# Hybrid decoder layer on one core: input-projection pairs placed ahead of the last three whole gates, PSUM pools closed one stage later, one more group of MLP operands made during the output projection

## The chip, the core and the metric

The kernel runs on one core of a Trainium2 chip. The core's engines work from queues of their own, each in order: TensorE (PE, matmuls; PEld is its weight load), VectorE (DVE), ScalarE (ACT), GpSimd (POOL) and SyncE (SP), which here issues every DMA. The metric is the device time of one execution in microseconds (us). Times inside an execution come from a profile of one execution, counted from its first instruction.

## The reference

One decoder layer over 1024 tokens, model width 1024, float32 in and out:

```python
h = h + hybrid_mixer(rms_norm(h, norm1_g), w_in, conv_w, conv_norm_g, ret_norm_g, w_out)
h = h + sq_relu_mlp(rms_norm(h, norm2_g), w_up, w_down)
return rms_norm(h, final_norm_g)
```

`hybrid_mixer` multiplies by `w_in` (1024 x 3584) and cuts the result into three convolution groups of 512 columns (b, c, h) and four retention groups of 512 (q, k, v, gate). The first give `b * causal_dwconv3(c * h)` and a group norm over 64 channels; the second a chunkwise retention in 4 heads of 128 with rotary q and k, a norm per head, and a product with `silu(gate)`. The 1024 columns that come out are multiplied by `w_out`. The MLP is `relu(u @ w_up)^2 @ w_down` with an inner width of 4096.

## The kernel before

Everything is kept transposed: 128 channels on the partitions, tokens along the row. Most tiles are 128 x 1024 float32 and come from one pool of 40 buffers ("units", `unit()`). A product in float32 precision is made of three products of rounded halves: an operand is split into a high half (ACT casts it) and a low half (DVE or POOL subtracts), and PE forms high x high, high x low and low x high. A piece of weights, 512 rows x 128 columns, is loaded by SP into a raw tile `r` (`Stream.fetch`, 4 buffers in the mixer), cast by ACT into `wh` and subtracted into `wl` (`split_piece`). `prepare()` does this for the next piece; it is called once per product or every other quarter of a whole tile, and pieces run four ahead of PE. `wh` and `wl` have 4 buffers each, so a cast can wait for PE to be done with an older piece. 12 matmuls of 128 x 512 make one product or one step.

The stages, with their places in the profiled execution: value projection and norm of the input (to 54 us); q and k tiles, then the first whole tiles, with the retention running beside them (to about 235 us); the pairs of input tiles (to 327 us); the last two gates, `IN_END` (to 350 us); the output projection (359 to 448 us); the first MLP products, `early` (448 to 496 us); six cycles of up and down products (to about 1031 us); the last down products and the final norm (to 1087 us).

Input tiles: numbers 0 to 11 are the convolution's (group i has 3i, 3i+1, 3i+2), 12 to 19 q and k, 20 to 23 the gates of heads 0 to 3. `whole(f)` makes one tile in 48 matmuls into two banks. `pair_in((f, g))` makes two tiles by seven block products instead of eight (a Strassen-like scheme, in the order `UP_ORDER`), 84 matmuls; it needs sums of weight blocks (`Left.split`, POOL) and sums of input blocks ("t1" to "t4", in `U`), and DVE adds each product from its bank into the outputs, seven additions in all. `use` then starts the rest for each half row: `conv_h`, `conv_b` with its norm (`norm`, two small matmuls with `blkr`), or `gate` (z * R, SiLU on ACT, product with the head's output).

The order of the background work is a planner's at build time: `now` counts PE's time in slots of 2.72 us, `clock` holds each engine's modelled end, and `background` emits a waiting task's next step once an engine would start it within `LOOK` = 3.2 us. PE's own order and `prepare` are fixed by the loops.

Because units are short, the outputs of heads 2 and 3 and the first two convolution outputs are written to DRAM (`put_by`, pool `spill`) and read back (`get_back`, tiles `back`) when the pairs are done. A task `split_y` waits for `y[idx]` (for idx 0 and 1 also for the key `("back", idx)`) and splits one half row into `y_h`, `y_l`. In `IN_END` the gates 22 and 23 are made first for half 0 and then for half 1, so that half 0 of all y can be split while half 1 is still on PE.

[...] The mixer has two pools of four, `pm` and `pr`; they belong to the `mixer` stack and are closed with it ahead of the output projection, where the pools `pu` (2), `pd` (4) and `pn` (2) are opened. `group(j)` makes output tiles j and 4 + j in eight steps: first half row 0 (both tiles, `w_out` rows 0 to 511, then 512 to 1023), then half row 1. `out_evac` adds the bank to the residual `x2`, squares it for the norm, and scales it into `un`. `todo` holds, by step number 8j + s, what is made for the MLP beside it: the seven operands "11", "21", "t1", "t3", "t2", "22", "t4" of each j (high half by ACT, low half by DVE), sums (`sum1` to `sum4`, DVE), `put_aside` (an `x2` tile to DRAM). For j = 0 and 1 all seven are made in the projection; for j = 2 and 3 the last four are made in `rest`, beside the 14 early products, which run in the order 11, 21, t2, t1, 22, t3, t4, each for two blocks. `fetch_back` reads tiles put aside, and `new_basis(i)` (POOL) subtracts part of `x2[i]` from `x2[i-1]` and `x2[i]`.

Nearly every DVE, ACT and POOL instruction is recorded under line 73, the call inside the planner's `Engine`; the profile tells them apart by their tiles.

Of the kernel before, what the change touches and what calls it, by code (L numbers as in the profile page):

```python
# [14 lines left out]
PSUM = bass.MemoryType.PSUM  # L15
# [21 lines left out]


IN_QK = [12, 13, 16, 17, 14, 15, 18, 19]
IN_TURNS = [0, 1, 2, 3, 20, (4, 5), (6, 7), 21, (8, 9), (10, 11)]  # L40
IN_END = [22, 23]
SLOT, LOOK, PE_MARGIN, LATE = 2.72, 3.2, 1.2, 0.0
NORM_MARGIN, STEP_MARGIN = 4.0, 0.3
# [35 lines left out]
def hybrid_layer(  # L79
# [16 lines left out]
    now, clock, procs, got = [0.0], {}, [], {}  # L96
    act = Engine(nc.scalar, 0.13, 0.95, now, clock)
    pool = Engine(nc.gpsimd, 0.2, 2.5, now, clock)
    dve = Engine(nc.vector, 0.13, 1.04, now, clock, pool)
# [4 lines left out]
    rw = ctx.enter_context(tc.tile_pool(name="rw", bufs=4))  # L104
    wp = ctx.enter_context(tc.tile_pool(name="wp", bufs=4))
    mixer = ctx.enter_context(ExitStack())
    pm = mixer.enter_context(tc.tile_pool(name="pm", bufs=4, space=PSUM))
    pr = mixer.enter_context(tc.tile_pool(name="pr", bufs=4, space=PSUM))
    tp = mixer.enter_context(tc.tile_pool(name="tp", bufs=6))
    xp = mixer.enter_context(tc.tile_pool(name="xp", bufs=1))  # L110

# [8 lines left out]
    def unit(dt=F32, s="u"):  # L120
        return big.tile([P, T], dt, tag="u", name=nm(s))
# [63 lines left out]
    IN_ORDER = list(IN_QK)  # L185
    for turn in IN_TURNS + IN_END:
        IN_ORDER += turn if isinstance(turn, tuple) else [turn]
# [37 lines left out]
    ahead = 3  # L225
    for turn in IN_TURNS + IN_END:
        if isinstance(turn, tuple):
            o = Left(mix, 1)
# [183 lines left out]
    def spawn(gen, ready=None, late=0.0):  # L412
        Task(gen, now[0] if ready is None else ready, late).go()
# [39 lines left out]
    def force(key):  # L453
        while key not in got:
            background(1e9)
            assert key in got, key

    y, y_h, y_l = [None] * KT, [None] * KT, [None] * KT
# [106 lines left out]
    o_n, retention_task = {}, [None, None]  # L565
# [165 lines left out]
    def whole(f):  # L731
        def evac(z):
            if f < 20 and f % 3 == 0:
                out = a_of[f // 3] = unit(s="a")
                for half, sl in enumerate(hs):
                    act.copy(out[:, sl], z[half])
                return
            out = None if f < 20 and f % 3 == 1 else unit(s="z")
            for half in range(2):
                spawn(use(f, half, out, z[half], True), clock[dve])  # L740

        tile_in(evac)
# [14 lines left out]
    def put_hi(name, j, src):  # L757
        u = unit(F32R, "U")
        act.copy(u[:, :H], src)
        U.setdefault(name, [None] * 4)[j] = (u[:, :H], u[:, H:])  # L760
# [93 lines left out]
    def put_by(key, of, *ready):  # L854
        for r in ready:
            yield r
        yield (dve,)
        t = of()
        spilt[key] = spill.tile([P, T], F32, tag="sp", name=nm("sp"))
        nc.sync.dma_start(spilt[key], t)  # L860
        mark(("by", key), dve)

    def get_back(key):
        t = unit(s="back")
        nc.sync.dma_start(t, spilt.pop(key))
        return t
# [12 lines left out]
        spawn(put_by(("o", h), lambda h=h: o_n[h, 0], ("o", h, 1)))  # L879
    for i in range(2):  # L880
        spawn(put_by(("y", i), lambda i=i: y[i], ("y", i, 0), ("y", i, 1)))
    for turn in IN_TURNS:
        if isinstance(turn, tuple):
            pair_in(turn)
        else:
            whole(turn)
    for h in (2, 3):
        force(("by", ("o", h)))
        o_n[h, 0] = o_n[h, 1] = get_back(("o", h))
    for i in range(2):  # L890
        force(("by", ("y", i)))
        y[i] = get_back(("y", i))
        got["back", i] = now[0] + 5.0
    for idx in range(KT):
        spawn(split_y(idx, 0))
    ends = {f: (unit(s="z"), [bank() for _ in hs], []) for f in IN_END}
# [32 lines left out]
        nc.sync.dma_start(x2[i], xT[i * P : (i + 1) * P, :])  # L929
    un = [None] * 4  # L930
    mixer.close()
    pm = ctx.enter_context(tc.tile_pool(name="pu", bufs=2, space=PSUM))
    pr = ctx.enter_context(tc.tile_pool(name="pd", bufs=4, space=PSUM))
    pn = ctx.enter_context(tc.tile_pool(name="pn", bufs=2, space=PSUM))
    ct = ctx.enter_context(tc.tile_pool(name="ct", bufs=11))
    kept = ctx.enter_context(tc.tile_pool(name="kept", bufs=5, space=bass.MemoryType.DRAM))
    rv = ctx.enter_context(tc.tile_pool(name="rv", bufs=8))
    temps.append(ct)

# [11 lines left out]
    def scaled(k, half):  # L951
        return x2[k][:, hs[half]], sm[:, G2 + k : G2 + k + 1]

    def put_scaled_hi(name, j, k, half):
        u = unit(F32R, "U")
        x, g = scaled(k, half)
        act.activation(u[:, :H], x, AF.Copy, scale=g)
        U.setdefault(name, [None] * 4)[j] = (u[:, :H], u[:, H:])
# [17 lines left out]
    def sum3(j):  # L976
        less(j, 1, un[j][:, hi_])
# [34 lines left out]
    def source(name, j):  # L1012
        return un[j][:, hi_ if name == "t3" else lo_]
# [13 lines left out]
    def group_todo(j):  # L1027

        hi_of = lambda *names: [lambda x=x: put_hi(x, j, source(x, j)) for x in names]
        lo_of = lambda *names: [lambda x=x: put_lo(x, j, source(x, j)) for x in names]  # L1030
        todo = {
            2: [lambda: put_scaled_hi("11", j, j, 0)],
            3: [lambda: put_scaled_lo("11", j, j, 0)],
            4: [lambda: put_scaled_hi("21", j, 4 + j, 0)],
            5: [lambda: put_scaled_lo("21", j, 4 + j, 0)],
            8: [lambda: sum1(j)] + hi_of("t1"),
            9: lo_of("t1") + [lambda: sum3(j)],
            10: [lambda: sum2(j)],
        }
        if j < 2:  # L1040
            todo[10] += hi_of("t3")
            todo[11] = lo_of("t3") + hi_of("t2")
            todo[12] = lo_of("t2") + [lambda: put_scaled_hi("22", j, 4 + j, 1)]
            todo[13] = [lambda: put_scaled_lo("22", j, 4 + j, 1), lambda: sum4(j)] + hi_of("t4")
            todo[14] = lo_of("t4")
            todo[15] = [lambda: put_aside(4 + j)]
        return todo

    def group(j):
        a, b = j, 4 + j  # L1050
        ws, banks = {}, {}
        steps = [(a, 0, 0), (b, 0, 0), (a, 1, 0), (b, 1, 0), (a, 0, 1), (b, 0, 1), (a, 1, 1), (b, 1, 1)]
        for s, (i, c, half) in enumerate(steps):
            if half == 0:
                ws[i, c] = parts.pop(0)
            elif j == 0:
                for idx in range(4 * c, 4 * c + 4):
                    force(("split", idx, 1))
            if c == 0:
                banks[i, half] = bank((pm, pr)[i == b])  # L1060
            mm(
                ws[i, c], [banks[i, half]],
                lambda n, k: (y_h[4 * c + k][:, hs[half]], y_l[4 * c + k][:, hs[half]]),
                c == 0, c == 1,
            )
            slot()
            if half:
                prepare()
            if c:
                out_evac(i, half, banks[i, half])  # L1070
            for t in todo.get(8 * j + s, []):
                t()
            if s == 2 and j in (1, 2):
                down.fetch(4)
            tick()

    todo = {}
# [3 lines left out]
    todo[16] += [lambda: new_basis(1)]  # L1081
    todo[17] += [lambda: put_aside(0), lambda: put_aside(1)]
    todo[24] += [lambda: put_aside(2)]
    todo[30] = [lambda: put_hi("t2", 2, source("t2", 2)), lambda: put_scaled_hi("22", 2, 6, 1)]
    for j in range(4):
        group(j)

    blocks = [w_up[p, i] for p in range(EARLY, NP_) for i in range(4)]
    blocks += [w_last[i] for i in range(KT)]
# [88 lines left out]
    def v_split(pairs, n, j):  # L1178
        c = pairs[j].c
        src = c[{1: "11", 2: "21", 3: "22", 4: "21", 5: "11", 6: "11", 7: "12"}[n]]  # L1180
        u = unit(F32R, "V")
        act.copy(u[:, :H], src)
        eng = pool if j and n not in (2,5) else dve
        eng.tensor_sub(u[:, H:], src, f32(u[:, :H]))
        V.setdefault(n, [None] * 2)[j] = (u[:, :H], u[:, H:])
# [18 lines left out]
    early = [Pair((pm, pr)[p]) for p in range(EARLY)]  # L1204

    def hi(name, *js):
        return [lambda j=j: put_hi(name, j, source(name, j)) for j in js]

    def lo(name, eng, *js):
        return [lambda j=j: put_lo(name, j, source(name, j), eng) for j in js]  # L1210

    def call(f, *js):
        return [lambda j=j: f(j) for j in js]
# [4 lines left out]
    def lo22(j):  # L1218
        put_scaled_lo("22", j, 4 + j, 1)

    rest = [
        todo[32] + lo("t2", dve, 2) + hi("t3", 2),
        todo[33] + call(lo22, 2) + todo[34] + call(hi22, 3) + hi("t2", 3),
        call(sum4, 2) + lo("t2", dve, 3) + hi("t3", 3) + lo("t3", dve, 2),
        call(sum4, 3) + call(lo22, 3) + hi("t4", 2, 3) + call(fetch_back, 0, 1),
        lo("t3", dve, 3) + call(fetch_back, 2, 4, 5),
        lo("t4", dve, 2),
        lo("t4", dve, 3),
        call(new_basis, 7),
        call(new_basis, 5),  # L1230
        call(new_basis, 3),
        [],
        [],
        [lambda: v_split(early, 1, 0)],
        [lambda: v_split(early, 1, 1)],
    ]
    for at, (n, p) in enumerate((n, p) for n in MLP_ORDER for p in range(EARLY)):
        b = early[p].product(n)
# [78 lines left out]
    for b in range(NBLK - 1):  # L1317
        new = [Pair(pm), Pair(pm)]
        todo = jobs(b, pairs, new)
# [193 lines left out]
```

## Time and profile before

| | us |
|---|---|
| median of 3 runs | 1090.49 (1089.0 to 1091.01) |
| the profiled execution | 1089.24 |
| its span, first to last instruction | 1087.5 |
| mean granted clock of TensorE | 0.991 |
| DMA moved, mean | 80.70 MB, 74 GB/s |

The profiled execution's own time is 1.7 us above its span. The page gives busy time per engine; a busy PE overlaps its matmuls (each is shown with about 0.39 us and the next starts 0.23 us later), so the distance between starts tells its pace. "Waits" name the instruction that sat idle and what released it. In the timeline each row has start, length, engine, line, operation, output <- inputs, count, and in brackets the idle time before it with its releaser.

### The profile page before, as it was taken

To read this page: it belongs to the slowest core of one execution; us is meant where nothing else is said; L and a number is where in the kernel's file an instruction comes from. 1 tells how busy PE (TensorE), PEld (TensorE's weight loads), DVE (VectorE), ACT (ScalarE), POOL (GpSimd) and SP (SyncE) were. 2 spreads that over 40 slices of the span, in tenths; PEclk is the share of its full clock that TensorE was granted. 3 is DMA by queue.
4 is the path that set the end of the run, shared out by engine and by line. 5 is a ranking of instruction groups with operands and counts; after the bars stand their busy time and mean duration, and the time that the engine had idled before them with its cause. 6 is when DMAs were issued, how large, how long until landed. Compare 5 with 4: busy or idle time off the path is not lost.

```text
span 1087.5 us, 13994 instructions
## 1 busy us (share of the span) xinstructions
PE 1056.8 (97%) x4916; PEld 881.0 (81%) x4916; DVE 873.3 (80%) x1256; ACT 469.8 (43%) x920; POOL 532.2 (49%) x368
## 2 busy tenths in 40 slices
PE   7999999999998799989999999999999999999996
PEld 6888888887887688878888888888888888888886
DVE  7436546798997556599999989989899899899945
ACT  8211445763446444444433343434343434334453
POOL 5234223255652223458538358267276295384543
PEclk9999999999999899999999999999999999999998
DMA  7111122212122625040121211202201301210204
GB/s 271 61 58 39 40 78 69 93 63 78 65 79 100 212 89 183 1 174 20 49 88 39 69 49 49 78 30 59 88 25 49 93 22 48 87 30 13 75 1 156
DMA packets 40022, 80.70 MB, mean 74 GB/s; under 512 B 4496, under 2 KB 6672, under 8 KB 39952
## 3 DMA queue, kind: packets, MB, share of 16 engines
q1 hardware_dynamic: 39952, 79.80, 22.6%
q8 instruction: 39, 0.64, 0.2%
q14 instruction: 31, 0.25, 0.1%
HBM read 70.87 MB, written 8.91 MB: 73 GB/s over the span
## 4 chain that ended last, share of the span: by engine, by line
PE 85%; DVE 6%; issue 4%; ACT 2%; DMA 2%; POOL 1%; SPq 0%; POOLq 0%; DVEq 0%; ACTq 0%
PE b L393 55%; PE b L1263 24%; PE b L349 2%; DVE wl L73 1%; DMA back<-sp 1%; DVE q L73 1%; DVE t L73 1%; PE b L330 1%; DMA xt<-xT 0%; PE b L613 0%; PE b L583 0%; ACT h L73 0%; PE b L651 0%; DVE z L73 0%; PE b L615 0%
## 5 line engine op out<-in xcount | busy, mean ns | idle before, releaser
L73 ACT CAST wh<-r 128x512 fp32r<-128x512 f32 x286 | 176.3, 621 | 336.0 <-PE b L393 141.2
L393 PE MATMUL b<-U,wh 128*128 128x512 f32 x1024 | 315.8, 389 | 3.0 <-DVE U L73 3.0
L73 DVE TENSOR_TENSOR wl<-r,wh 128x512 fp32r<-128x512 f32 x247 | 225.4, 915 | 97.1 <-ACT wh L73 96.4
L73 POOL TENSOR_TENSOR r<-r,r 128x512 f32<-128x512 f32 x136 | 208.7, 1537 | 120.9 <-DVE wl L73 69.9
L1263 PE MATMUL b<-V,wh 128*128 128x512 f32 x784 | 241.8, 389 | 0.4 <-POOL V L73 0.4
L393 PEld LDWEIGHTS b<-U,wh 128*128 128x128 f32 x1024 | 192.0, 188 | 43.2 <-DVE U L73 3.4
L73 DVE TENSOR_TENSOR x<-x,b 128x512 f32<-128x512 f32 (+1 forms) x320 | 198.0, 665 | 27.6 <-PE b L393 24.7
L393 PE MATMUL b<-U,wl 128*128 128x512 f32 x512 | 199.3, 389 | 0.0
L1263 PEld LDWEIGHTS b<-V,wh 128*128 128x128 f32 x784 | 147.1, 188 | 31.8 <-POOL V L73 0.8
L73 POOL TENSOR_TENSOR t<-t,t 128x512 f32<-128x512 f32 x70 | 105.6, 1513 | 102.3 <-ACT t L73 56.3
L1263 PE MATMUL b<-V,wl 128*128 128x512 f32 x392 | 152.5, 389 | 0.0
L73 POOL TENSOR_TENSOR wl<-r,wh 128x512 fp32r<-128x512 f32 x39 | 56.2, 1446 | 160.9 <-ACT wh L73 154.4
L393 PEld LDWEIGHTS b<-U,wl 128*128 128x128 f32 x512 | 96.1, 188 | 20.5 <-POOL wl L73 0.4
L393 PE MATMUL b<-uh,wh 128*128 128x512 f32 x304 | 102.1, 396 | 0.0
L393 PE MATMUL b<-uh,wl 128*128 128x512 f32 x304 | 100.3, 390 | 1.7 <-DVE wl L73 1.7
L393 PE MATMUL b<-ul,wh 128*128 128x512 f32 x304 | 100.4, 390 | 0.0
L1263 PEld LDWEIGHTS b<-V,wl 128*128 128x128 f32 x392 | 73.6, 188 | 15.2
L73 POOL TENSOR_TENSOR V<-t,V 128x512 fp32r<-128x512 f32 x35 | 49.7, 1421 | 67.2 <-ACT V L73 67.1
L73 DVE TENSOR_TENSOR t<-t,b 128x512 f32<-128x512 f32 x112 | 76.0, 678 | 1.7 <-POOL t L73 1.2
L73 ACT ACTIVATE t<-t 128x512 f32<-128x512 f32 x64 | 40.2, 631 | 73.3 <-DVE t L73 72.6
L73 DVE TENSOR_TENSOR V<-t,V 128x512 fp32r<-128x512 f32 x63 | 69.3, 1100 | 0.0
L393 PEld LDWEIGHTS b<-uh,wl 128*128 128x128 f32 x304 | 57.1, 188 | 14.2 <-DVE wl L73 2.1
(163 smaller groups left out, 1422.0 us busy)
## 6 DMA issues: line engine op xcount, KB each, us to landing
r<-w_up_t SPq DMA_DIRECT2D x64, 256.0 KB, 2.6
r<-w_down_t SPq DMA_DIRECT2D x56, 256.0 KB, 2.6
r<-w_in_t SPq DMA_DIRECT2D x48, 256.0 KB, 2.7
xt<-xT SPq DMA_DIRECT2D x16, 256.0 KB, 5.4
xs<-xT SPq DMA_DIRECT2D x8, 512.0 KB, 4.8
r<-w_out_t SPq DMA_DIRECT2D x16, 256.0 KB, 2.6
x<-xT SPq DMA_DIRECT2D x8, 512.0 KB, 7.3
outT<-out SPq DMA_DIRECT2D x6, 512.0 KB, 2.8
```

The costliest lines, as they stand in the source:

```text
L73: return f(out, *args, **kw)
L330: nc.tensor.matmul(b[:, c * P : (c + 1) * P], d, ident, start=True, stop=True)
L349: nc.tensor.matmul(vb[i], a[k][:, tsl], b[k // 2][:, vs], start=(k == 0 and a is uh and b is vh), stop=(k == KT - 1 and a is ul),)
L393: nc.tensor.matmul(b, a[:, k, :], rhs(n, k)[r], start=(start and i == 0), stop=(stop and i == len(ops) - 1),)
L1263: nc.tensor.matmul(b, a, r, start=(i == 0), stop=(i == len(ops) - 1))
```

## The change

Three things. First, `IN_TURNS` is reordered: the pairs (8, 9) and (10, 11) now come straight after (6, 7), and gate 21, which stood between (6, 7) and (8, 9), comes after them, ahead of gates 22 and 23. The four tiles in DRAM are now read back before gate 21 instead of after the last turn (which was the pair (10, 11)), so at the same point of the pairs' work; the planner's time for the returned y is 10 us later instead of 5. The order in which the pieces of `w_in` are loaded follows `IN_TURNS`.

Second, the pools `pm` and `pr` move from the `mixer` stack to a stack of their own, `banks_`, which is closed after the output projection; `pu`, `pd` and `pn` are opened there. The output projection uses four plus four banks instead of two plus four.

Third, for j = 2 the operands t3, t2, 22 and t4 are made in the projection, like those of j = 0 and 1, and `x2[6]` is put aside too (pool `kept` 6 buffers instead of 5). `rest` loses them, and its remaining steps for j = 3 move up; two steps `v_split` move up by two products.

```diff
-IN_TURNS = [0, 1, 2, 3, 20, (4, 5), (6, 7), 21, (8, 9), (10, 11)]
+IN_TURNS = [0, 1, 2, 3, 20, (4, 5), (6, 7), (8, 9), (10, 11), 21]
...
-    pm = mixer.enter_context(tc.tile_pool(name="pm", bufs=4, space=PSUM))
-    pr = mixer.enter_context(tc.tile_pool(name="pr", bufs=4, space=PSUM))
+    banks_ = ctx.enter_context(ExitStack())
+    pm = banks_.enter_context(tc.tile_pool(name="pm", bufs=4, space=PSUM))
+    pr = banks_.enter_context(tc.tile_pool(name="pr", bufs=4, space=PSUM))
...
-    for turn in IN_TURNS:
+    for at, turn in enumerate(IN_TURNS):
         if isinstance(turn, tuple):
             pair_in(turn)
         else:
             whole(turn)
-    for h in (2, 3):
-        force(("by", ("o", h)))
-        o_n[h, 0] = o_n[h, 1] = get_back(("o", h))
-    for i in range(2):
-        force(("by", ("y", i)))
-        y[i] = get_back(("y", i))
-        got["back", i] = now[0] + 5.0
+        if at == len(IN_TURNS) - 2:
+            for h in (2, 3):
+                force(("by", ("o", h)))
+                o_n[h, 0] = o_n[h, 1] = get_back(("o", h))
+            for i in range(2):
+                force(("by", ("y", i)))
+                y[i] = get_back(("y", i))
+                got["back", i] = now[0] + 10.0
...
     mixer.close()
-    pm = ctx.enter_context(tc.tile_pool(name="pu", bufs=2, space=PSUM))
-    pr = ctx.enter_context(tc.tile_pool(name="pd", bufs=4, space=PSUM))
-    pn = ctx.enter_context(tc.tile_pool(name="pn", bufs=2, space=PSUM))
     ct = ctx.enter_context(tc.tile_pool(name="ct", bufs=11))
-    kept = ctx.enter_context(tc.tile_pool(name="kept", bufs=5, space=bass.MemoryType.DRAM))
+    kept = ctx.enter_context(tc.tile_pool(name="kept", bufs=6, space=bass.MemoryType.DRAM))
...
-        if j < 2:
+        if j < 3:
             todo[10] += hi_of("t3")
...
-    todo[30] = [lambda: put_hi("t2", 2, source("t2", 2)), lambda: put_scaled_hi("22", 2, 6, 1)]
     for j in range(4):
         group(j)
+    banks_.close()
+    pm = ctx.enter_context(tc.tile_pool(name="pu", bufs=2, space=PSUM))
+    pr = ctx.enter_context(tc.tile_pool(name="pd", bufs=4, space=PSUM))
+    pn = ctx.enter_context(tc.tile_pool(name="pn", bufs=2, space=PSUM))
...
     rest = [
-        todo[32] + lo("t2", dve, 2) + hi("t3", 2),
-        todo[33] + call(lo22, 2) + todo[34] + call(hi22, 3) + hi("t2", 3),
-        call(sum4, 2) + lo("t2", dve, 3) + hi("t3", 3) + lo("t3", dve, 2),
-        call(sum4, 3) + call(lo22, 3) + hi("t4", 2, 3) + call(fetch_back, 0, 1),
-        lo("t3", dve, 3) + call(fetch_back, 2, 4, 5),
-        lo("t4", dve, 2),
-        lo("t4", dve, 3),
+        todo[32] + call(hi22, 3),
+        todo[33] + todo[34] + hi("t2", 3),
+        lo("t2", dve, 3) + hi("t3", 3) + call(lo22, 3),
+        call(sum4, 3) + lo("t3", dve, 3) + hi("t4", 3) + call(fetch_back, 0, 1),
+        lo("t4", dve, 3) + call(fetch_back, 2, 4, 5, 6),
+        [],
+        [],
         call(new_basis, 7),
...
+        [lambda: v_split(early, 1, 0)],
+        [lambda: v_split(early, 1, 1)],
         [],
         [],
-        [lambda: v_split(early, 1, 0)],
-        [lambda: v_split(early, 1, 1)],
     ]
```

## The prediction

> **What bounds the kernel now.** I read the page first, then the view of PE's waits, then the granted clock by windows, then the timeline at each hole of PE.
>
> ```profile
> PE 1056.8 (97%) x4916; PEld 881.0 (81%) x4916; DVE 873.3 (80%) x1256; ACT 469.8 (43%) x920; POOL 532.2 (49%) x368
> ...
> PE b L393 <- DVE z L73: 9.1, 1, 9.1
> PE b L393 <- DVE U L73: 3.0, 1, 3.0
> PE b L393 <- DVE wl L73: 1.7, 1, 1.7
> ```
>
> TensorE (PE) is the bound, and the change leaves its 4916 matmuls as they are. So only the 30.7 us in which PE is idle (1087.5 span less 1056.8) and slow clock can be won. Three waits lie where the change works: 9.1 us, 3.0 us and 1.7 us. The timeline of PE gives their places, and one row of the chain gives the pitch: 13.61/60 = 0.227 us a matmul.
>
> ```profile
> 227.22 13.61 PE b L393 x60
> ...
> 349.71 0.39 PE L393 MATMUL b<-uh,wl 128*128 128x512 f32 x1
> 359.23 0.77 PE L393 MATMUL b<-yh,wh 128*128 128x512 f32 x1 [9.13 <-DVE z L73]
> ...
> 362.63 0.40 PE L393 MATMUL b<-yh,wl 128*128 128x512 f32 x1
> ...
> 462.66 0.40 PE L393 MATMUL b<-U,wh 128*128 128x512 f32 x1
> 466.02 0.50 PE L393 MATMUL b<-U,wh 128*128 128x512 f32 x1 [2.96 <-DVE U L73]
> ```
>
> Seam 1 is between input projection and output projection. PE could go on at 349.71 + 0.23 = 349.94 and starts at 359.23: 9.29 us lost. Then eight intervals to 362.63 take 3.40 us instead of 8 x 0.227 = 1.81: 1.59 more. Together 10.9. Seam 2 is the early MLP's fifth product: 466.02 - 462.66 - 0.23 = 3.1. The windows (length, PE busy, clock, DMA share, GB/s) show why only seam 1 has a slow tail:
>
> ```profile
> 350.00:359.00 9.00, 0.10 (x1) 0.62 0.24 69
> 359.00:363.00 4.00, 3.77 (x10) 0.57 0.91 301
> ...
> 463.00:466.00 3.00, 0.05 (x1) 1.00 0.00 0
> 466.00:480.00 14.00, 13.98 (x70) 1.00 0.71 260
> ```
>
> A gap of 9.29 us drops the clock, one of 3.1 us does not.
>
> **Part 1, seam 1.** The first product of group(0) needs a PSUM bank, the split halves of y[0..3], and the first split piece of w_out. The timelines of SP, ACT, POOL and DVE show when each came:
>
> ```profile
> 331.53 1.86 SPq L865 DMA_DIRECT2D back<-sp  x4
> ...
> 340.44 0.62 ACT L73 CAST yh<-back 128x512 fp32r<-128x512 f32 x1 [0.64 <-DMA back<-sp]
> ...
> 346.81 0.69 ACT L73 ACTIVATE r<-b,eps 128x512 f32<-128x512 f32 x1
> ...
> 351.93 3.13 POOL L73 TENSOR_TENSOR wl<-r,wh 128x512 fp32r<-128x512 f32 x2 [8.39 <-ACT wh L73]
> ...
> 354.46 1.15 DVE L73 TENSOR_TENSOR yl<-z,yh 128x512 fp32r<-128x512 f32 x1
> ...
> 358.41 0.68 DVE L73 TENSOR_TENSOR z<-b,R 128x512 f32<-128x512 f32 x1
> ```
>
> The bank came last: the new pools opened only when gate 23's last bank had been read (358.41 + 0.68 = 359.09), and PE followed 0.14 later. The split of y[3] was there at 355.61, the first piece at about 353.5. So keeping the banks by itself moves PE to about 355.7, a gain of 3.5. The rest must come from the order. ACT, in order, sat on the returned tiles until 340.44, and the roots of the last convolution's norm, queued behind, came only from 346.81 on. With tile 21 behind the last pair, that pair's tail and the four return loads are 48 x 0.227 = 10.9 us further ahead of the end of the projection: the split of y[3] falls at 355.6 - 10.9 = 344.7, before 349.94. Can DVE carry it? The windows give its load (third busy column):
>
> ```profile
> 277.20:288.10 10.90, 10.90 (x50) 9.03 (x49) 10.68 (x12) 2.60 (x5) 8.01 (x6) 1.00 0.13 50
> 288.10:327.05 38.95, 38.95 (x174) 32.26 (x172) 35.03 (x41) 18.06 (x29) 21.33 (x15) 1.00 0.23 68
> 327.05:349.94 22.89, 22.89 (x102) 18.77 (x100) 15.13 (x22) 13.66 (x21) 4.41 (x3) 1.00 0.33 116
> ...
> 293.27 1.28 DVE L73 TENSOR_TENSOR z<-b,R 128x512 f32<-128x512 f32 x2
> 294.65 1.41 DVE L73 SCALAR_TENSOR_TENSOR q<-z,sm,q 128x512 f32<-128x512 f32 x2
> ```
>
> Tile 21 ran from 277.2 to 288.1. Without its own 2.7 us (the last two rows) DVE has 10.68 + 35.03 - 2.7 = 43.0 us of work for the two pairs' 38.95 us, and 4.1 us run over. From there to the end of the projection PE needs 10.9 + 22.9 = 33.8 us; DVE has 15.1, at most the 8.5 between 349.94 and 358.41, 2.7 and 4.1: 30.4. It fits, by 3.4 us, and the last halves need not be ready at the start. I take the whole 10.9; the other end is 3.5.
>
> **Part 2, what the move costs.** Pairs now follow each other without the light tile between them. PE waited once at such a border, (4,5) to (6,7), and the chain shows how:
>
> ```profile
> 252.14 4.09 DMA r<-w_in_t
> ...
> 256.39 1.40 POOL r L73
> ...
> 257.81 0.63 ACT wh L73
> ...
> 258.47 1.23 DVE wl L73
> ...
> 262.58 0.68 DVE L73 TENSOR_TENSOR z<-z,b 128x512 f32<-128x512 f32 x1
> ...
> 267.78 0.50 PE L393 MATMUL b<-uh,wl 128*128 128x512 f32 x1 [1.68 <-DVE wl L73]
> ...
> 283.93 0.68 DVE L73 TENSOR_TENSOR z<-z,b 128x512 f32<-128x512 f32 x1
> ...
> 312.34 0.67 DVE L73 TENSOR_TENSOR z<-z,b 128x512 f32<-128x512 f32 x1
> ```
>
> The three DVE rows drain the last product of (4,5), (6,7) and (8,9), which PE ended at 254.7, 277.2 and 307.56 (each pair is 7 x 12 matmuls, 19.04 us, counted back from 327.05 with the small norm matmuls between): DVE is 7.9, 6.7 and 4.8 us behind. At 7.9 PE waited 1.68, at 4.8 (border to (10,11)) nothing. The new border (6,7) to (8,9) has 6.7: by the straight line 1.68 x 1.9/3.1 = 1.0. Ends: nothing, and 1.68 at both pair borders, 3.4. What waits behind a late weight split is only PE itself and its drains.
>
> **Part 3, the new bank wait.** The pools of the MLP now open after the last evacuation of the output projection, and behind that wait stands all of PE. In before this border had no gap:
>
> ```profile
> 447.89 0.62 PE L393 MATMUL b<-U,wh 128*128 128x512 f32 x2
> ...
> 448.28 0.60 ACT L73 CAST U<-un 128x512 fp32r<-128x512 f32 x1
> 448.79 0.72 ACT L73 ACTIVATE U<-x,sm 128x512 fp32r<-128x512 f32 x1
> ...
> 450.90 0.68 DVE L73 TENSOR_TENSOR x<-x,b 128x512 f32<-128x512 f32 x1
> ```
>
> The last evacuation ended at 451.58, 3.69 after 447.89; with 0.1 for the signal, 3.8. It stood behind a weight split whose cast waited for the two U casts at 448.28 and 448.79. These move ahead (1.2 us), which leaves 2.6. No row shows whether a new bank waits for all old ones or only for the one in its place; the latter would cost nothing, so the ends are 0 and 3.8. I take 2.6, since seam 1 was released by the very last bank.
>
> [...]
>
> **Part 4, operands ahead.** Seam 2 waited for t2's low half of group 3, on DVE behind three operations for group 2, sum4 among them:
>
> ```profile
> 463.54 0.75 DVE L73 SCALAR_TENSOR_TENSOR un<-x,sm,un 128x512 f32<-128x512 f32 x1
> ```
>
> Low t2, low "22" and sum4, at 0.7 each 2.1, leave the queue ahead of it. The operand is then due at 466.0 - 2.1 = 463.9, while PE, held 2.6 by Part 3, asks for it at 462.9 + 2.6 = 465.5. Weight casts in between wait for PE's products, so some of the 2.6 reaches the operand; if all did, 1.0 of the wait would stay. I let the 3.1 go. The moved work (five DVE operations, four casts, about 3.5 and 2.6 us) lies in the last group beside PE, where DVE is busy 11.23 of 20 us:
>
> ```profile
> 420.00:440.00 20.00, 20.00 (x90) 16.55 (x89) 11.23 (x16) 7.57 (x13) 5.18 (x5) 1.00 0.23 82
> 481.84 1.30 POOL L73 TENSOR_TENSOR x<-x,x 128x512 f32<-128x512 f32 x1 [9.31 <-DMA x<-k]
> ```
>
> The 40 units are full there (16 y halves, 3 x2, 2 un, 19 operands), so ACT may stand until y's first units are freed, two steps later; behind it wait weight casts that PE needs three steps later, so it costs nothing, and if that cover fails it lengthens Part 3's wait. The sixth tile put aside adds two transfers of 512 KB on SP, and new_basis(7) on POOL now waits for its return as new_basis(5) did (second row); behind it stand only the other basis sums. The two v_split steps come two products sooner, beside PE. Nothing for both.
>
> **Sum.** -10.9 + 1.0 + 2.6 - 3.1 = -10.4. The profiled execution took 1089.24 (span 1087.5 and 1.7 around it), which gives 1078.8; it lies 1.25 under the median of the runs, 1090.49, and against the median I forecast **1080.1**.
>
> **Rivals.**
> (a) The MLP's banks do not wait for all: -10.9 + 1.0 - 3.1, **1077.5**. For it: nothing but seam 1 shows the rule. Against: there the releaser was the last of four banks.
> (b) The order brings nothing forward and only the banks count: -3.5 + 2.6 - 3.1, **1086.5**. For it: DVE fits by only 3.4 us. Against: ACT's wait for returned tiles is visible and goes.
> (c) The bank wait is at its 3.8 and the clock falls, with seam 1's 1.59 after it: -10.9 + 1.0 + 3.8 + 1.6 - 3.1, **1082.9**. For it: POOL's weight sums run there too. Against: the two casts leave.
> (d) Slower: the chain of Part 2 (load 4.09, sum 1.40, cast 0.63, split 1.23 = 7.35, less one product of 2.72 as cover, 4.6) stands exposed at all three borders after (6,7), 13.9: -10.9 + 13.9 + 2.6 - 3.1, **1093.0**. It decides from 3.8 us a border, 11.4 in all, where it eats the other terms. Against: the worst so far is 1.68.
> (e) The change does not do what it says: the new pools' wait simply moves, as long as before, from seam 1 to the MLP, and the order helps nothing. -10.9 + 9.3 + 1.6 at no gain elsewhere, **1090.5**. Against: by 447.89 the drains of DVE trail by 3.8, not 9.3.
>
> **Chances.** Forecast 0.58, (a) 0.15, (b) 0.10, (c) 0.10, (d) 0.04, (e) 0.03. The range takes in the forecast, (a) and (c), 0.83: from (a) with nothing lost at the pair borders, 1076.5, less 1 us for the spread of the runs (1089.0 to 1091.01), 1075.5; to the forecast with every cost at its upper end (2.4 more in Part 2, 1.2 and 1.6 in Part 3), 1085.3, so 1085.5. A measurement of this kernel can tell about 0.2%, 2.2 us: faster 0.93, same 0.03, slower 0.04.
>
> **What would show it.** Step 1: no wait of PE between b<-uh and b<-yh, clock 1.00 there. Step 2: waits of PE on wl between 277 and 316, about 1 us in all. Step 3: a wait of the first early product on DVE x, about 2.6. Step 4: no wait on U. Wrong if PE waits on wl by more than 3 us in the pairs, or y's splits still end after the projection.

## The result, and the profile after

The changed kernel took 1084.65 us (median of 4 runs, 1083.79 to 1085.01), against 1090.22 for the kernel before in the same comparison: a ratio of 0.995, with a 95% interval of 0.9937 to 0.9962. The forecast was 1080.1, the range 1075.5 to 1085.5. So the sign and the range held, and the gain was 5.6 us where 10.4 were forecast.

The page of the changed kernel shows the same bound, PE, with as many matmuls as before:

```profile
span 1082.8 us, 13995 instructions
...
PE 1058.5 (98%) x4916; PEld 880.3 (81%) x4916; DVE 878.6 (81%) x1254; ACT 463.7 (43%) x916; POOL 538.5 (50%) x370
```

The span went from 1087.5 to 1082.8, by 4.7. The view of PE's waits has lost the 9.1 on z and the 3.0 on U; a list of smaller ones has come in their place (columns: who waits and for whom, total, times, longest):

```profile
PE b L394 <- DVE z L73: 2.3, 1, 2.3
PE b L394 <- DVE wl L73: 1.2, 1, 1.2
...
PE b L394 <- DVE x L73: 1.2, 2, 0.7
PE b L394 <- DVE t L73: 1.1, 1, 1.1
...
PE b L474 <- ACT s L73: 1.0, 1, 1.0
PE b L394 <- ACT t L73: 0.7, 1, 0.7
```

The timeline, here of PE, DVE, ACT and POOL in order of start, gives each its place:

```profile
296.72 0.50 PE L474 MATMUL b<-s,blkr 128*128 128x512 f32 x1 [0.96 <-ACT s L73]
297.44 0.50 PE L475 MATMUL b<-s,blkr 128*128 128x512 f32 x1 [0.22 <-DVE s L73]
...
318.37 2.19 DVE L73 TENSOR_TENSOR z<-z,b 128x512 f32<-128x512 f32 x3
320.61 0.50 PE L394 MATMUL b<-uh,wh 128*128 128x512 f32 x1 [2.29 <-DVE z L73]
...
355.45 0.39 PE L394 MATMUL b<-uh,wl 128*128 128x512 f32 x1
355.68 0.39 PE L394 MATMUL b<-yh,wh 128*128 128x512 f32 x1
...
435.21 0.63 ACT L73 CAST U<-un 128x512 fp32r<-128x512 f32 x1 [1.82 <-PE b L394]
...
442.52 0.68 DVE L73 TENSOR_TENSOR x<-x,b 128x512 f32<-128x512 f32 x1
443.35 0.70 PE L394 MATMUL b<-U,wh 128*128 128x512 f32 x2 [0.47 <-DVE x L73]
446.19 0.67 DVE L73 TENSOR_TENSOR x<-x,b 128x512 f32<-128x512 f32 x1
447.01 0.70 PE L394 MATMUL b<-U,wh 128*128 128x512 f32 x2 [0.69 <-DVE x L73]
...
476.80 1.30 POOL L73 TENSOR_TENSOR x<-x,x 128x512 f32<-128x512 f32 x1 [13.17 <-DMA x<-k]
486.94 5.04 POOL L73 TENSOR_TENSOR r<-r,r 128x512 f32<-128x512 f32 x3
509.12 0.70 PE L394 MATMUL b<-U,wh 128*128 128x512 f32 x2 [1.08 <-DVE t L73]
526.93 0.70 PE L394 MATMUL b<-U,wh 128*128 128x512 f32 x2 [0.73 <-ACT t L73]
```

Seam 1 is gone: the first matmul on y starts 0.23 after the last one on u. New holes are to be seen: at a norm's small matmuls in the pairs (296.72), at gate 21 (320.61), twice at the first early products (443.35, 447.01), and in the first block of the MLP (509.12, 526.93). The one at gate 21 also cost clock, as the windows show (length, busy time of PE, PEld, DVE, ACT and POOL with counts, clock, DMA share, GB/s):

```profile
317.82:321.24 3.42, 1.12 (x6) 0.61 (x5) 3.25 (x5) 0.00 (x0) 0.08 (x1) 1.00 0.36 111
321.24:324.65 3.41, 3.41 (x10) 2.65 (x9) 2.55 (x4) 1.75 (x3) 1.30 (x2) 0.50 0.00 0
```

To see where the time went I set the start of every matmul of the changed kernel beside that of the matmul with the same number of the kernel before. Both run the same number, and how much a difference grows over a stretch is what the stretch gained or lost; where the order differs only the ends of the stretch count:

| stretch | forecast | measured |
|---|---|---|
| to the border of the first two pairs | 0 | -1.2 |
| pairs from there, and gate 21 | +1.0 | +6.9 |
| seam 1 | -10.9 | -10.9 |
| border to the MLP | +2.6 | +1.6 |
| seam 2 | -3.1 | -3.05 |
| first MLP block | 0 | +2.6 |
| the rest | 0 | -0.25 |
| together | -10.4 | -4.3 |

The span shrank by 0.4 more, behind the last matmul. The first row is not in a part that was edited: 0.8 of it is there by 235 us, where runs 4 and 6, the same up to there, had 0.3 and 0.5; the other 0.4 is at the weight split of before, where it waited 1.23 and those runs 1.68. So it is the spread of single executions. The 6.9 is made of 0.3 at a weight split, 1.7 at the norm's matmuls of 296.72, 0.6 at those of 306.69, 2.55 at gate 21's bank and 1.7 of half clock behind it.

### The profile page after: what moved, and what is told of

Its sections match the earlier page's. It is cut to its first block, busy times and chain, and to the rows that moved or that the text cites. A ratio compares the mean times of both kernels' runs of the same rounds, so it can differ in the third digit from the quotient of the medians.

```text
span 1082.8 us, 13995 instructions
## 1 busy us (share of the span) xinstructions
PE 1058.5 (98%) x4916; PEld 880.3 (81%) x4916; DVE 878.6 (81%) x1254; ACT 463.7 (43%) x916; POOL 538.5 (50%) x370
## 4 chain that ended last, share of the span: by engine, by line
PE 81%; DVE 8%; POOL 4%; issue 3%; DMA 1%; ACT 1%; POOLq 0%; DVEq 0%; SPq 0%; ACTq 0%
PE b L394 51%; PE b L1265 22%; PE b L350 4%; DVE wl L73 2%; POOL r L73 1%; POOL z L73 1%; DVE z L73 1%; DVE x L73 1%; DVE t L73 1%; DMA x<-k 1%; DVE q L73 1%; POOL x L73 1%; DVE V L73 1%; PE b L305 0%; PE b L614 0%
## 5 line engine op out<-in xcount | busy, mean ns | idle before, releaser
L73 DVE TENSOR_TENSOR wl<-r,wh 128x512 fp32r<-128x512 f32 x251 | 232.1, 927 | 91.7 <-ACT wh L73 90.8
L73 POOL TENSOR_TENSOR wl<-r,wh 128x512 fp32r<-128x512 f32 x35 | 49.0, 1407 | 160.6 <-ACT wh L73 156.8
```

What stands on the lines that cost most here:

```text
L73: return f(out, *args, **kw)
```

## The experiments

Each was timed beside the kernel before (medians of 1090.53, 1090.35 and 1090.21 us in the three groups: the first three runs and the fourth; the fifth to eighth; the last four).

| run | median, us | ratio to before, 95% |
|---|---|---|
| the change | 1084.65 | 0.9937 to 0.9962 |
| 1 order alone | 1090.08 | 0.9985 to 1.0002 |
| 2 banks alone | 1083.55 | 0.9917 to 0.9942 |
| 3 operands alone | 1090.33 | 0.9987 to 1.0005 |
| 4 change, gate 21's second bank | 1082.76 | 0.9915 to 0.994 |
| 5 the same, norm margin 8 | 1079.28 | 0.9887 to 0.9914 |
| 6 change, x2[3] aside | 1081.24 | 0.9908 to 0.9936 |
| 7 banks and operands | 1082.38 | 0.9918 to 0.9943 |
| 8 change with 4, 5 and 6 | 1077.72 | 0.9868 to 0.9899 |
| 9 run 7 with 5 and 6 | 1084.16 | 0.9929 to 0.9958 |
| 10 run 8, norm margin 12 | 1074.57 | 0.984 to 0.9869 |
| 11 change, look-ahead 1.6 | 1091.36 | 1.0001 to 1.0018 |
| 12 run 8, look-ahead 1.6 | 1095.63 | 1.0034 to 1.0061 |

### 1 The order alone

The kernel before with the first third of the diff only (`IN_TURNS`, and the tiles read back before the last turn).

> Theory: the new order alone keeps its price and most of its gain. In the changed kernel's trace PE loses 6.9 us in the pairs and at gate 21 (2.5 waiting for a bank at gate 21, 1.7 in half clock behind it, 2.3 at the norm's small matmuls, 0.4 at a weight split), and the last read of gate 23's bank ends 2.8 us after the projection. So with the pools closed at the old place: pairs +6.5, seam 1 shrinks from 9.3 + 1.6 to 2.8 (-8.1, or -6.5 if the clock falls again), seam 2 stays at 3.1. Together about -1.6 us, 1088.6. Rival: the waits in the pairs come from the banks being kept, not from the order; then they are absent here and the time is about 1082.

Measured 1090.08, no difference from before. In the pairs it loses the same 6.9 as the change, and PE's timeline shows the old bank wait standing in for what the order won at seam 1:

```profile
321.74 0.79 PE L393 MATMUL b<-uh,wh 128*128 128x512 f32 x1 [2.32 <-DVE z L73]
359.52 0.76 PE L393 MATMUL b<-yh,wh 128*128 128x512 f32 x1 [2.58 <-DVE z L73]
```

The clock fell behind both: the two matmuls took 0.79 and 0.76, where the one behind the wait at 320.61 in the change took 0.50 at full clock. Counted by matmuls it won 6.6 at the seam. So the order by itself pays for its gain in full, and the cost in the pairs belongs to it and not to the other two edits.

### 2 The banks alone

```diff
+    banks_ = ctx.enter_context(ExitStack())
-    pm = mixer.enter_context(tc.tile_pool(name="pm", bufs=4, space=PSUM))
-    pr = mixer.enter_context(tc.tile_pool(name="pr", bufs=4, space=PSUM))
+    pm = banks_.enter_context(tc.tile_pool(name="pm", bufs=4, space=PSUM))
+    pr = banks_.enter_context(tc.tile_pool(name="pr", bufs=4, space=PSUM))
...
         group(j)
+    banks_.close()
```

> Banks kept, old order, operands as before. Theory: PE starts the output projection when y[3] is split, at about 355.7 instead of 359.2 (-3.5), the clock still falls there; at the MLP a new bank waits only for the old one in its place, 1 to 3 us, of which the fifth product's wait of 3.1 gives part back because PE comes later. About -2 us, 1088.2. Rival: a new bank waits for all old ones; then the border costs 3.8 and the result is about 1090.

Both numbers were missed: it took 1083.55, a gain of 7.0, more than the 5.6 of all three parts together (the two intervals just overlap). The timelines of PE and ACT at the seam:

```profile
349.86 0.39 PE L394 MATMUL b<-uh,wl 128*128 128x512 f32 x1
...
352.36 0.60 ACT L73 CAST wh<-r 128x512 fp32r<-128x512 f32 x1
353.01 0.50 PE L394 MATMUL b<-yh,wh 128*128 128x512 f32 x1 [2.77 <-ACT wh L73]
353.40 0.62 ACT L73 CAST yh<-z 128x512 fp32r<-128x512 f32 x1 [0.44 <-DVE z L73]
...
354.56 0.50 PE L394 MATMUL b<-yh,wl 128*128 128x512 f32 x1 [0.81 <-POOL wl L73]
```

PE starts at 353.01, as soon as the first piece of w_out is cast, and 0.39 before the last half of y is even cast. A product takes its four blocks of y one after the other, three matmuls each, so y[3] is not needed before the tenth matmul. The start came 6.2 earlier than before's 359.23 in this place, not 3.5; the wait at 354.56 and 3.4 us of half clock took some of it back, and by its end the seam had gained 5.1.

### 3 The operands alone

The third part only: `if j < 3`, `kept` with 6 buffers, the new `rest`.

> Only the third group's operands made ahead, and its tile put aside. Theory: the fifth product's wait (3.1) goes and three waits in the first block (2.6 in the changed kernel) come, because GpSimd's first basis sum stands waiting for the sixth returned tile and the weight sums of the first block stand behind it: -0.5 us, 1089.7. Rival: the first block's waits come from the moved bank wait; then they are absent and the time is 1087.1.

Measured 1090.33: nothing, about as the theory had it. Seam 2 gained 1.8 and kept a wait of 1.2 on U, and two waits in the first MLP block, 0.89 on DVE t and 0.73 on ACT t, came with it and took the gain back. They stand here without the order and the banks, so they belong to this part.

### 4 Gate 21's second bank from the other pool

A whole tile takes two banks of `pm`. After the pair (10, 11) the second of them is one that DVE drains late. It is not the last product's: counting a pair's seven additions in order, the three in the row at 318.37 above are the two that follow the fourth product and the one of the fifth, and the last product's comes only at 327.20, when PE has long gone on. The fifth product's addition ends this row at 320.56, 8.1 after that product's last matmuls made way for the next at 312.49, and PE starts 0.05 later. This run takes the second bank from `pr` for a whole gate behind the pairs, which is gate 21 alone.

```diff
-        out = [bank() for _ in hs]
+        out = [bank(), bank(pr if got.get("pairs") else pm)]
```

> The changed kernel, with the second bank of the whole gate after the pairs taken from pr instead of pm. Theory: gate 21's wait of 2.5 us was for its second bank of pm, held by a product that VectorE drains 8 us late, and the half clock of 1.7 us came from that gap; both go: -4.1 against the changed kernel, 1080.5. Rival: VectorE is simply late, and PE stands at the next thing it needs from it (a low half of weights or the next bank); then less than 1.5 us come back, 1083 or more.

Measured 1082.76, 1.9 less than the change (the two intervals just overlap), between the theory's 1080.5 and the rival's 1083, and nearer to the rival. The hole at gate 21 and the half clock are gone, 4.2 in the trace; but the last pair's norm matmuls, which PE now reaches sooner, wait in their turn, and 2.6 are lost there:

```profile
330.73 0.49 PE L474 MATMUL b<-s,blkr 128*128 128x512 f32 x1 [0.87 <-ACT s L73]
331.45 0.50 PE L475 MATMUL b<-s,blkr 128*128 128x512 f32 x1 [0.23 <-DVE s L73]
...
332.78 0.50 PE L475 MATMUL b<-s,blkr 128*128 128x512 f32 x1 [0.22 <-DVE s L73]
```

Here the late engines showed up at the next thing that PE asked of them, for 2.6 of the 4.2.

### 5 The same, with the norm's matmuls asked for later

`norm` puts its two small matmuls into PE's queue once the planner's time is `NORM_MARGIN` microseconds past the end it models for the squares. ACT and DVE are further behind the planner than 4.0, so PE meets them too soon: in run 4 it waited for 0.87 on ACT s and 0.23 on DVE s at 330.73 and 331.45.

```diff
-NORM_MARGIN, STEP_MARGIN = 4.0, 0.3
+NORM_MARGIN, STEP_MARGIN = 8.0, 0.3
```

> The changed kernel with gate 21's second bank from pr (as in the run before, 1082.8) and the planner's margin ahead of the norm's small matmuls at 8 us instead of 4. Theory: VectorE and ScalarE run about 8 us behind in the pairs, so PE meets these matmuls before their input is cast; in that run it waited 2.3 us at 297 to 308 and 2.4 us at 330 for them. With 8 us both go: -4.7 against it, 1078.1. Rival: the loss belongs to VectorE's load and not to the place of the small matmuls; then PE stands at weight splits or at the seam instead, and the time is 1081 or more.

Measured 1079.28, 1.2 above the theory. The norm's waits at 297 to 308 are gone, of those at 330 one of 1.1 on ACT s and one of 0.2 are left. Not all of the gain lies there. Counted by matmuls this trace is 4.3 ahead of run 4's, and 2.7 of it is there before the pair (8, 9) begins: 0.2 by 235 us, and most of the rest at two waits that the kernel before has too, of 1.68 on a weight split (now 0.44) and of 0.23 at a norm. In the two moved pairs only 1.0 is won, because a weight split at 301 now waits 0.86; at 330 it is 0.6.

### 6 Another tile put aside

`put_aside` writes an `x2` tile of each of the first groups to DRAM; with three groups it writes x2[4], x2[5], x2[6], and `new_basis(7)`, the first of POOL's basis sums, needs x2[6], the last one to come back. Here x2[3] goes in its place, and 4 and 5 are fetched first.

```diff
-            todo[15] = [lambda: put_aside(4 + j)]
+            todo[15] = [lambda: put_aside(4 + j if j < 2 else 3)]
...
-        lo("t4", dve, 3) + call(fetch_back, 2, 4, 5, 6),
+        lo("t4", dve, 3) + call(fetch_back, 4, 5, 2, 3),
```

> The changed kernel with x2[3] put aside and read back in place of x2[6], so that GpSimd's first basis sum (tiles 6 and 7) waits for no transfer. Theory: the three waits in the first block (2.6 us) come from GpSimd standing 13 us for x2[6], with the first block's weight sums behind it; they go, 1084.65 - 2.6 = 1082.0. Rival: they come from the V split on GpSimd, which the change put ahead of these weight sums; then at least 1.5 us of them stay, 1083.5 or more.

Measured 1081.24, and the waits in the first block are gone; one of 0.31 came at 467. The V split still stands ahead of the weight sums (481.36), so the rival fell. Not all of the gain is theirs: in this trace the wait at gate 21, 2.27, did not drop the clock, and that is worth 1.7 (see the last section). POOL's timeline tells why the first block's waits went: it starts the sums that wait for a return 4.2 sooner (PE is 0.5 ahead of the change there), four of them and not six, and comes to the weight sums 4.3 sooner:

```profile
472.60 1.30 POOL L73 TENSOR_TENSOR x<-x,x 128x512 f32<-128x512 f32 x1 [7.09 <-DMA x<-k]
...
482.61 3.12 POOL L73 TENSOR_TENSOR r<-r,r 128x512 f32<-128x512 f32 x2
```

### 7 Everything but the order

> The changed kernel with the old order of tiles and return loads (banks kept, operands ahead). Banks alone gave 1083.55. Theory: the order gives at the seam what it takes in the pairs: here the seam costs about 5.7 us as with banks alone, the pairs nothing, the fifth product's rest of 1.9 goes and the first block's 2.6 comes: 1084.2, no more than 0.1% from the changed kernel. Rival: with all three parts the order is needed; then the time is 1087 or more.

Measured 1082.38, by the medians 2.3 less than the change (the two intervals just overlap): the rival fell, and the order seems to cost 0.2%, where the theory had 0.1% at most. PE starts the output projection at 350.71 with waits of 1.0 on the cast of w_out and 0.8 on its low half, and the clock falls for 3.4 us. Counted by matmuls this seam gains 6.9 without the order and 10.9 with it; the order adds 4.0 here and takes 6.9 in the pairs. The 6.9 without the order is not a firm number: run 2 runs the same instructions up to the seam and gained 5.1. ACT got the last returned tile later there, run 2 first, then run 7:

```profile
341.56 0.62 ACT L73 CAST yh<-back 128x512 fp32r<-128x512 f32 x1 [0.64 <-DMA back<-sp]
...
339.25 0.62 ACT L73 CAST yh<-back 128x512 fp32r<-128x512 f32 x1 [0.63 <-DMA back<-sp]
```

In the old order the seam hangs on that return; against run 2 the order adds 5.8.

### 8 The change with all three mends

> The changed kernel with all three mends: gate 21's second bank from pr, margin 8 us, x2[3] put aside in place of x2[6]. Theory: the mends add, since they lie at different places: 1084.65 - 1.9 - 4.7 - 2.6 = 1075.4. Rival: they do not add, because what PE waited for at one place is VectorE's total load; then 1079 or more.

Measured 1077.72: beats the kernel before by 1.0% to 1.3%. That is between theory and rival: the mends take 6.9 off the change, where the theory had 9.2. Left in its trace are norm waits of 1.1 and 0.2 at 330.95 and 331.68, weight splits of 0.4 and 0.9, and the MLP's border.

### 9 The mends without the order

Run 7 with `NORM_MARGIN` 8.0 and x2[3] put aside.

> The order of before, with the banks kept, the operands made ahead, a norm margin of 8 slots and x2[3] put aside instead of x2[6]: the run that combined all mends, without the order. Theory (the order is worth little once its costs are mended): the run with banks and operands in the old order took 1082.4; the waits in the first block go (2.6, as measured when x2[3] was put aside), the norm's waits near 267 to 272 go (up to 2), and the seam keeps its two waits of 1.0 and 0.8 and its slow clock of 1.7: about 1078, within 2 us of the 1077.7 of the run with the order. Rival (the order is worth its 10.9 less what the banks alone gave): 1081 or more, 3 us or more above the run with the order.

(The margin counts microseconds of the planner's time, not slots.) Measured 1084.16: the theory fell, the rival's number came true. Timelines of ACT and PE at the seam:

```profile
349.80 0.69 ACT L73 ACTIVATE r<-b,eps 128x512 f32<-128x512 f32 x1
...
355.94 0.62 ACT L73 CAST yh<-z 128x512 fp32r<-128x512 f32 x1 [1.09 <-DVE z L73]
...
356.61 0.79 PE L394 MATMUL b<-yh,wh 128*128 128x512 f32 x1 [4.82 <-ACT yh L73]
```

In run 7 the same root stands at 345.61. A norm that is asked for 4 us later makes y[3] later, and with the pair (10, 11) next to last there is no room for it: PE waits 4.82 at the tenth matmul, and the clock is at half until 361.82. With the order the same margin costs nothing at the seam. In run 8 ACT's timeline has the last cast of that half of y here:

```profile
344.65 0.62 ACT L73 CAST yh<-z 128x512 fp32r<-128x512 f32 x1 [1.01 <-DVE z L73]
```

That is 11.3 sooner than in run 9, and 6.4 before PE's first matmul on y (351.07). So the order's worth depends on what uses the room: with a margin of 4.0 it costs 2.3 (the change against run 7), with 8.0 it brings 6.4 (run 8 against run 9, where run 8 has gate 21's bank changed as well).

### 10 A still later norm

Run 8 with `NORM_MARGIN` 12.0.

> The run that combined all mends, with the norm margin at 12 slots instead of 8. Theory (the two waits left at 329 to 331.7, together about 1.9, are small norm matmuls that still come before ScalarE and VectorE have made their squares, because the engines run further behind the planner than 8 slots): they go, about 1076. Rival (a norm asked for later makes y later, and the output projection waits for it): 1077.7 or more, with a wait of PE between the two projections.

Measured 1074.57, the best of all, 1.3% to 1.6% below the kernel before. From 240 us to the end of the input projection PE waits once, for a weight split, and there is no wait at the seam:

```profile
span 1072.8 us, 13996 instructions
...
PE 1054.8 (98%) x4916; PEld 880.2 (82%) x4916; DVE 871.9 (81%) x1254; ACT 466.7 (44%) x918; POOL 536.8 (50%) x370
...
299.89 0.50 PE L394 MATMUL b<-U,wl 128*128 128x512 f32 x1 [1.29 <-DVE wl L73]
```

### 11 and 12 A shorter look-ahead

`LOOK` 1.6 instead of 3.2, in the change and in run 8: is VectorE late because background steps stand ahead of the drains, or because there is too much of them?

```diff
-SLOT, LOOK, PE_MARGIN, LATE = 2.72, 3.2, 1.2, 0.0
+SLOT, LOOK, PE_MARGIN, LATE = 2.72, 1.6, 1.2, 0.0
```

> The changed kernel with the planner's look-ahead at 1.6 us instead of 3.2, nothing else. Theory (VectorE is some 8 us behind in the pairs because background steps are put in its queue ahead of the drains of the pairs' banks; a shorter look-ahead puts fewer in): most of the 6.9 lost in the pairs and gate 21 goes, about 1080. Rival (the lag is load, not order: VectorE has 43 us of work for 39 us of matmuls): the waits stay where they are or move, 1084 or more.

> The run that combined all mends, with the look-ahead at 1.6 us as well. Theory (lag by order): a little better than 1077.7, about 1076.5. Rival (lag by load, and a shorter look-ahead leaves engines idle elsewhere): 1077.7 or more.

Measured 1091.36 and 1095.63, 6.7 and 17.9 more than without it, both on the rivals' side by the number. But the loss begins at another place, ahead of the first pair (timelines of ACT and PE of run 11); run 12 has the same one, and a wait for y at the seam besides:

```profile
244.95 0.61 ACT L73 ACTIVATE t<-z 128x512 f32<-128x512 f32 x1
245.65 0.62 ACT L73 CAST s<-t 128x512 fp32r<-128x512 f32 x1
...
246.32 0.79 PE L474 MATMUL b<-s,blkr 128*128 128x512 f32 x1 [7.87 <-ACT s L73]
...
254.62 0.79 PE L394 MATMUL b<-U,wh 128*128 128x512 f32 x1 [2.21 <-ACT U L73]
```

Here the square for a norm comes late in ACT's queue; PE stands 7.87, and the clock is at half from 243.06 for 17.07 us. Beside the kernel before PE is 15.0 behind at 260 us; it then loses nothing more in the pairs. But by then DVE has had all that time to catch up, so the question of order or load stays open. What is shown is only that the look-ahead can't be halved for all stages at once.

## Why the prediction came out as it did

**Range and sign right, the gain too large.** In the traces 4.3 was gained and 10.4 forecast, 6.1 too much. Part 2 had 5.9 too little cost and Part 4 2.6; Part 3 had 1.0 too much, 1.2 were won ahead of the pairs, and the rest is small. The medians differ by less (1084.65 against 1080.1), because the profiled execution of before lies 1.25 under its median and the span shrank by 0.4 more behind the last matmul. That the time lies within the range is in part luck: the range's upper end allowed for 2.4 more at the weight splits and 2.8 at the MLP's border, and neither came; what filled that room were costs the prediction did not name.

**Part 1, seam 1: the size right, the shares wrong.** 10.9 forecast, 10.9 measured, with clock 1.00 and no wait, as said. But "keeping the banks by itself moves PE to about 355.7, a gain of 3.5" is refuted by run 2: 353.01. The step took the whole of y as due at the first matmul, where the product's own order makes y[3] due ten matmuls in; the first piece of w_out bound instead. The order was left with 4.0 to 5.8 of the 10.9, not 7.4. Rival (b) has the order bring nothing forward, and that fell: alone it wins 6.6 at the seam (run 1) and gives it back in the pairs. What the order is worth on balance is near what (b) says, but the banks' share at the seam is 5.1 to 6.9 (runs 2 and 7), not 3.5.

**Part 2: the term that was mis-sized, 1.0 against 6.9.** The step looked for the cost at the pair borders and in one mechanism, the late weight split. That cost 0.3. It had the cause in hand, DVE 7.9, 6.7 and 4.8 behind, and followed it to one consumer only. The others that the same lag reaches are the norm's small matmuls, which the planner sets by its own time (2.3), and gate 21's second bank, which the late drain of the pair's fifth product frees (2.55, and 1.7 of clock). Run 4 shows the second by taking it away, runs 5 and 10 the first; some of what they took away came back at other places, as said there.

The lag that was priced was also the wrong one, though the right one was at hand. Part 1 works out that DVE runs 4.1 over in the two pairs, and uses it for the seam alone; Part 2 takes 6.7, the lag of the old border. The drain of the last product of (10, 11) in before; then, in the change, those of (8, 9) and of (10, 11):

```profile
331.94 0.68 DVE L73 TENSOR_TENSOR z<-z,b 128x512 f32<-128x512 f32 x1
```

```profile
305.41 0.68 DVE L73 TENSOR_TENSOR z<-z,b 128x512 f32<-128x512 f32 x1
...
327.20 0.68 DVE L73 TENSOR_TENSOR z<-z,b 128x512 f32<-128x512 f32 x1
```

PE ended (10, 11) at 327.05 and at 317.93: DVE was 4.9 behind and is 9.3 behind, 4.4 more. The straight line from lag to weight split does not hold either: PE ended (8, 9) at 295.60, so DVE was 9.8 behind at that border, and no weight split waited there. For gate 21 the fifth product counts. Before, where gate 21 stood behind (6, 7), its drain was the third of this row and ended at 275.38, 1.8 ahead of PE's first matmul of that gate (277.20), so PE did not wait:

```profile
273.19 2.19 DVE L73 TENSOR_TENSOR z<-z,b 128x512 f32<-128x512 f32 x3
```

Rival (c) had a fall of the clock, but at the MLP's border, where it didn't come. No run shows a bank wait of 3.8 there, or what it would do to the clock: the change's two were 0.47 and 0.69, at full clock.

**Part 3: 2.6 against 1.6.** The two ends had been a wait for all banks (3.8) and for each place alone (0). The timeline after shows the second: the first early product starts at 443.35, 0.15 after the drain that ended at 443.20 (442.52 + 0.68), though another of the old banks is drained only at 446.86; and the second product starts 0.15 after that one. The price is not nothing, because the first two banks of the new pools lie where late drains were. So neither the forecast nor rival (a) had it whole.

**Part 4: 3.1 right, a zero wrong.** Seam 2 went as forecast, 3.05. But "Nothing for both" failed for `new_basis(7)`: behind it stand, in POOL's queue, not "only the other basis sums" but the weight sums of the next stage. POOL stood 13.17 and its six sums ended at 485.7; the weight sums came at 486.94 where before they came at 487.87, and PE, 6.8 ahead there, found them 5.9 later by its own time. Run 3 shows that the cost belongs to this part, run 6 that the late return was its cause. The full units that the prediction named were there too (ACT stood 1.82 for a product at 435.21), and hid as it said.

Rivals (d) and (e) fell: the chain of load, sum, cast and split was not exposed, and the new pools' wait did not move whole.

## What to carry to other kernels

When an engine is found to run late, list everything that PE takes from it in that stretch, not only the one that waited before: weight splits, banks to be freed, small matmuls that a planner times by its model. An order that brings work forward makes room, and room is worth something only when a margin uses it; try the two together, since apart each may measure as nothing or as a loss. When a product is due, its first operand is due, not its last: count matmuls to the operand that is late before pricing the wait.

## What the hardware showed that was not expected

The prediction said that a gap of 9.29 us drops the clock and one of 3.1 does not. The change itself refutes the rule: its gap of 2.3 at gate 21 dropped it, and run 6's gap of 2.27 in the same place did not. In the traces of before and of the change the granted clock changes only at distances that are multiples of 3.413 us: before, it was half from 352.19 to 362.43, 3 times that, and whole from there to 1079.23, 210 times; in the change half from 321.24 to 324.65, once, and whole from there to 1075.58, 220 times. Run 9 had half clock for 6.83 and run 11 for 17.07, 2 and 5 times. By windows of that length, the clock went with PE's busy time in the one window before, and not with the length of the gap. The windows are cut on this grid, first those of before, then of run 6:

```profile
348.78:352.19 3.41, 1.32 (x6) 0.75 (x4) 3.34 (x7) 3.04 (x4) 0.26 (x1) 1.00 0.00 0
...
461.42:464.83 3.41, 1.63 (x8) 0.98 (x6) 1.90 (x3) 3.02 (x6) 1.12 (x1) 1.00 0.00 0
464.83:468.24 3.41, 2.22 (x10) 1.84 (x11) 3.41 (x5) 0.11 (x1) 0.98 (x2) 1.00 0.27 77
```

```profile
316.78:320.20 3.42, 2.07 (x10) 1.38 (x8) 3.35 (x4) 0.00 (x0) 1.63 (x1) 1.00 0.54 153
320.20:323.61 3.41, 2.49 (x11) 2.08 (x12) 2.45 (x5) 1.06 (x2) 0.00 (x0) 1.00 0.10 37
```

Seam 2's longer gap was cut in two by the grid, 1.63 and 2.22 busy, and so was run 6's; the change's 2.3 lay in one window, 1.12 busy, and the next ran at half. Of the windows at full clock between 240 and 560 us, these with 1.49 busy or less were followed by half clock: 0.00 (run 11), 0.21 (run 9), 1.11 and 1.13 (run 1), 1.12 (the change), 1.32 (before), 1.46 (run 12) and 1.49 (run 2). These with 1.63 or more were not: 1.63, 2.22, 2.49 and 2.65 (before), 1.75 (run 2), 2.07 (run 6), 2.19, 2.33 and 2.48 (the change). Between them it went both ways: 1.54 in run 3 kept it, and 1.59 in run 7, with two waits of 1.0 and 0.8, lost it. So for these stages an estimate from the last two puts the point near 1.55 of 3.41, about 45% busy. It is no general figure: busy time is counted as the profile shows it, and at the end of the kernel, where some matmuls have one column only, windows with 1.94 (before) and 1.65 (the change) busy were followed by half clock as well.

A hole of PE therefore cost its own length here, and the change's hole of 2.3, which fell into one window, cost another 1.7. How the grid lies to the program differs from trace to trace: one window begins at 317.82 in the change, and at 316.78 in run 6, whose instructions are the same up to there.
